# Hybrid SSD / MLA / PEER block on one core: one gate multiplication per build step, and a later decode of the gathered token block

## The chip, the cores and the metric

The kernel runs on one core of a Trainium2 chip. The engines of the core are named as the profile names them: PE (TensorE, the matrix engine; PEld is its weight load), DVE (VectorE), ACT (ScalarE), POOL (GpSimd) and SP (SyncE, which here only issues DMAs). Each engine works through its own queue of instructions in order; they wait for each other through semaphores. The metric is the time of one execution on the device in microseconds, as the median of several runs.

## The reference

The model is one decoder layer for 512 tokens of width 1024: a layer norm, a mixer (16 state-space heads and 8 latent-attention heads, one input and one output projection), a second layer norm, and then the expert mixer that the change is about, followed by a third layer norm. The expert mixer, for a block of 128 tokens:

```python
q = (xb @ w_query).reshape(T, PEER_HEADS, 2, PEER_HALF_DIM)
s = jnp.einsum('thkd,hknd->thkn', q, sub_keys)
sv, si = lax.top_k(s, K)                              # K = 16 of 128, per head and half
cand_s = (sv[:, :, 0, :, None] + sv[:, :, 1, None, :]).reshape(T, PEER_HEADS, K * K)
cand_i = (si[:, :, 0, :, None] * PEER_N_KEYS + si[:, :, 1, None, :]).reshape(T, PEER_HEADS, K * K)
top_s, top_pos = lax.top_k(cand_s, K)
expert_idx = jnp.take_along_axis(cand_i, top_pos, axis=-1)
gate = jax.nn.softmax(top_s, axis=-1)
act = jax.nn.gelu(jnp.einsum('td,thkd->thk', xb, u_table[expert_idx]), approximate=False)
return jnp.einsum('thk,thkd->td', gate * act, v_table[expert_idx])
```

Each token so picks 8 x 16 = 128 of 16384 experts; expert number = 128 i + j, where i and j are the two sub-key numbers.

## The kernel before

The tokens are four blocks of 128. For blocks 0 to 2 the kernel does not gather expert rows: it multiplies all 16384 rows of both tables densely. For block 3 it gathers the picked rows from memory. The expert mixer runs in these stages.

1. **Queries and top-16** (`w_query_fm`, `sub_scores`, `stage1`, `top16`). DVE finds the 16 best sub-keys and then the 16 best candidates of every head; the results for all four blocks lie in `TS4` (scores), `PO4` (positions among the candidates) and `TI4` (sub-key numbers).
2. **Decode** (`stage2`). From a position DVE computes the pair of ranks (a, b), looks up the sub-key numbers i and j with a comparison against the table `iaE`, a multiplication with the numbers and four halving additions (L1018 to L1026, once per block, in the order 2, 0, 1, 3), and computes the softmax gate. The result of block b is `IJG[b]`: i, j and gate.
3. **Gate build** (`build_g`, 48 steps for blocks 0 to 2, eight tokens each). The wanted thing is a matrix G[expert, token] with the gates at the picked places. For one token it is the product of a one-hot matrix of j with a one-hot matrix of i that is scaled by the gates. `g_head(b)` transposes i, j and gate on PE and writes them as fp16, the gate as a high part and a low part. `hot(n)` makes the one-hots of step n on DVE with one comparison (L1111, 2048 elements per partition), multiplies the i one-hots by the low gates into `g1` (L1115, 1024 elements) and by the high gates in place (L1116, 1024 elements). PE multiplies (L1134, L1135; 16 matmuls of 128x128 a step), ACT copies the result to `stg`, and every fourth step SP writes `stg` to the DRAM buffers `gs0` and `gsp`. The one-hots of two steps and `g1` are double-buffered, and `hot(n + 1)` is issued ahead of the matmuls of step n.
4. **u and v chunks**. Chunk c is 128 experts. A *u chunk* (`u_chunk`) is the product of 128 rows of the u table with the activations of blocks 0 to 2, in three passes of split precision (`mm3`, L72 to L74; 24 matmuls), and a gelu on ACT. A *v chunk* (`v_chunk`) multiplies by G (`v_prep`, L1325, G read back through `gt`), splits the product in a high and a low part (`v_hi`, L1338; `v_lo`, L1345), and adds its 18 matmuls (L1354 to L1358) into six accumulators that stay in PSUM. The weights of both come as 512 KB pieces through `Stream`: SP loads a piece into one of three `wir` buffers, ACT rounds it to a high part (L109), DVE subtracts to get the low part (L119, "the weight split"); there are three buffers of the low part.
5. **Gather for block 3** (`gather`). POOL gathers, for each of the 128 picks, one row of u and later one row of v per token (L1391); DVE does a dot product with each u row (L1402) and adds each v row, scaled, to `ac` (L1408). It ends with the block's layer norm.

The stages overlap by a plan that is made while the program is written out. Up to 54 u chunks (`LEAD`) may be done early, their results kept in SBUF. `drive(fill)` keeps two clocks: `tm[0]` for PE (4.07 per u chunk, 1.1 per build step) and `tm[1]` for DVE (the numbers that `stage2` and `build_g` yield, and 1.2 per weight split). It puts a u chunk in as long as PE's clock is not ahead of DVE's and fewer than 52 chunks (`LEAD - RES`) are out, and otherwise takes the next piece of the filler, `stage2` or `build_g`. Sixteen tokens of block 2 are treated like block 3 for their u side: their 16 rows of u (`urow`) are multiplied on DVE in between the build steps (`ug_dots`, L1056). Chunks that are left of the 54 come behind the build. Then the main loop issues one u chunk and one v chunk at a time while u chunks remain, then v chunks alone. In each round `pump` takes pieces of `gather` worth a given time; once rows are gathered, their number follows the work that is left, so that the rows end a fixed distance before the end.

DMAs of SP go out in the order of the program and SP waits in that order; so do the instructions of each engine.

Of the kernel before, what the change touches and what calls it, by code (L numbers as in the profile page):

```python
# [53 lines left out]
def tile_block(ctx: ExitStack, tc: tile.TileContext, I, out):  # L54
# [921 lines left out]
    def stage2():  # L976
        f4 = lambda z: z.rearrange("p b h k -> p (b h k)")
        g4 = lambda z: z.rearrange("p b h k -> p (b h) k")
        d = rt2.tile([128, NB, 8, 16], F32, name="dd")
        sm = rt2.tile([128, NB * 8], F32, name="smm")  # L980
        V.tensor_tensor(g4(d), g4(TS4), g4(TS4)[:, :, 0:1].to_broadcast([128, NB * 8, 16]), op=OP.subtract)
        sm_ = lambda n, dt=F32: rt2.tile([128, NB * 128], dt, name=n)
        p3, p2, pf, a1, af, b1 = sm_("p3", U32), sm_("p2", U32), sm_("pf"), sm_("a1"), sm_("af"), sm_("b1")
        abf = rt2.tile([128, NB, 2, 128], F16, name="abf")
        ti = rt2.tile([128, NB, 2, 8, 16, 2], F16, name="tif")
        pos = f4(PO4)
        ab = lambda e: abf[:, :, e]
        v4 = lambda z: z.rearrange("p (b k) -> p b k", b=NB)
# [3 lines left out]
        yield 1.6  # L992
# [4 lines left out]
        yield 1.7  # L997
# [5 lines left out]
        yield 2.6  # L1003
# [3 lines left out]
        for b in range(NB):  # L1007
            IJG[b] = ijp.tile([128, 3, 8, 16], F32, name="ijg", bufs=4)
            V.tensor_tensor(IJG[b][:, 2], d[:, b], sm[:, b * 8:(b + 1) * 8, None].to_broadcast([128, 8, 16]), op=OP.mult)
        yield 2.0  # L1010
        sh = [128, 16, 16, 16]
        for b in (2, 0, 1, 3):
            for c in range(2):
                A.activation(ti[:, b, :, :, :, c].rearrange("p e h a -> p h e a"),
                             TI4[:, b].rearrange("p (h e) a -> p h e a", e=2), AF.Copy)
            eq = rt2.tile([128, 16, 16, 16], F16, name="eq")
            abv = abf[:, b].rearrange("p e (h k) -> p (e h) k", k=16)
            V.tensor_tensor(eq, abv[:, :, None, :].to_broadcast(sh), iaE[:, None].to_broadcast(sh), op=OP.is_equal)  # L1018
            yield 2.3
            eqv = eq.rearrange("p g a (k c) -> p (g a) k c", c=2)  # L1020
            tv = ti[:, b].rearrange("p e h a c -> p (e h a) c")
            V.tensor_tensor(eqv, eqv, tv[:, :, None, :].to_broadcast([128, 256, 8, 2]), op=OP.mult)
            yield 2.3
            for w in (8, 4, 2):
                V.tensor_tensor(eq[:, :, :w], eq[:, :, :w], eq[:, :, w:2 * w], op=OP.add)
            V.tensor_tensor(IJG[b][:, 0:2].rearrange("p e h k -> p (e h) k"), eq[:, :, 0], eq[:, :, 1], op=OP.add)  # L1026
            yield 2.8
            if b == 2:
                ug_index(p3)
            if b == 1:  # L1030
                g_head(0)

# [33 lines left out]
    def ug_head():  # L1066
# [15 lines left out]
        A.activation(gT[:, 0, 128 - UG:], ps[:, :UG], AF.Copy, scale=GSC)  # L1082
        yield 0.1
        V.scalar_tensor_tensor(gT[:, 1, 128 - UG:], ps[:, :UG], GSC, gT[:, 0, 128 - UG:],
# [3 lines left out]
    def g_head(b):  # L1088
        ijg = IJG.pop(b)
        ps = px()  # L1090
        for e in range(3):
            T.transpose(ps[:, e * 128:(e + 1) * 128], ijg[:, e].rearrange("p h k -> p (h k)"), ident)
        ijT = ijp.tile([128, 16, 2, 8], F16, name="ijT", bufs=2)
        gT = ijp.tile([128, 2, 128], F16, name="gT", bufs=2)
        A.activation(ijT.rearrange("p n e t -> p e n t"),
                     ps[:, 0:256].rearrange("p (e n t) -> p e n t", e=2, t=8), AF.Copy)
        A.activation(gT[:, 0], ps[:, 256:384], AF.Copy, scale=GSC)
        V.scalar_tensor_tensor(gT[:, 1], ps[:, 256:384], GSC, gT[:, 0], op0=OP.mult, op1=OP.subtract)
        GT[b] = ijT, gT

    def build_g():
        bc = [128, 4, 128, 2]

        def hot(n):
            ijT, gT = GT[n // 16]
            t0 = n % 16 * 8
            col = lambda z: z[:, t0:t0 + 8].rearrange("p (q c) -> p q c", c=2)[:, :, None, :].to_broadcast(bc)
            ij = gb.tile([128, 2, 4, 128, 2], F16, name="ij", bufs=2)
            g1 = gb.tile(bc, F16, name="g1", bufs=2)
            b2 = [128, 8, 128, 2]  # L1110
            V.tensor_tensor(ij.rearrange("p e q i c -> p (e q) i c"), iotaE[:, None].to_broadcast(b2),  # L1111
                            ijT[:, n % 16].rearrange("p e (q c) -> p (e q) c", c=2)[:, :, None, :].to_broadcast(b2),
                            op=OP.is_equal)
            oi, oj = ij[:, 0], ij[:, 1]
            V.tensor_tensor(g1, oi, col(gT[:, 1]), op=OP.mult)  # L1115
            V.tensor_tensor(oi, oi, col(gT[:, 0]), op=OP.mult)  # L1116
            return oj, oi, g1
# [5 lines left out]
        for n in range(48):  # L1123
# [25 lines left out]
            yield 2.55 if n < 47 else 0.1  # L1149
# [70 lines left out]
    iaE = ijp.tile([128, 16, 16], F16, name="iaE")  # L1220
    nc.sync.dma_start(iotaE.rearrange("p a b -> p (a b)"), I["ch"][:, 0:256])
    nc.sync.dma_start(iaE.rearrange("p a b -> p (a b)"), I["ch"][:, 256:512])
# [60 lines left out]
    rt2 = pool("rt2")  # L1283
    lo_on[0] = V
# [85 lines left out]
    def gather():  # L1370
        ijg = IJG.pop(3)
# [5 lines left out]
        close(ijp)  # L1377
# [56 lines left out]
    while vc <= LASTC:  # L1434
# [11 lines left out]
        if GS[0] < 0:  # L1446
            more = pump(fill, 1.7 * w)
# [153 lines left out]
```

## Time and profile before

| | |
|---|---|
| median of 3 runs | 1629.04 us (1628.13 to 1629.44) |
| profiled execution, its own time | 1628.98 us |
| its span, first to last instruction | 1627.1 us |
| PE busy | 1584.2 us (97%) |
| PE weight load busy | 1395.5 us (86%) |
| DVE busy | 1363.0 us (84%) |
| ACT busy | 704.9 us (43%) |
| POOL busy | 465.7 us (29%) |
| moved by DMA | 394.82 MB, mean 243 GB/s |

In the rows of the profile, `L1111` is line 1111 of the kernel before, then come engine, operation, and output<-inputs by the names of the tiles (shortened, and without buffer numbers: `ij` is the one-hot tile, `g` the tile `g1`, `wih` and `wil` the high and low parts of the weights, `va` the accumulators). A row of the timeline begins with the start and the duration in us; in square brackets stands how long the engine had been idle and what ended the wait. The decode lies at 549 to 600 us of the profiled execution, the build at 600 to 785, the first v chunk at 799, the gathered rows from 818 to 1550.

### The profile page before, as it was taken

The page shows a single profiled execution, that of the slowest core. Times are in us where ns is not written, and L with a number is a line of the kernel's source. Part 1 is how long each engine was busy: PE and PEld are TensorE (multiplying, and loading weights), DVE is VectorE, ACT ScalarE, POOL GpSimd, SP SyncE. Part 2 cuts the span into 40 slices and gives each one's busy share as a digit, 9 for nine tenths or more (in the row PEclk, how much of TensorE's full clock was granted, in tenths as well). Part 3 has the DMA queues.
Part 4 walks back from the last instruction along what each step waited for, and adds up shares of the span by engine and source line. Part 5 has one row for each costly group of instructions (what it writes and reads, how often), then busy time and mean ns, then how long its engine had stood idle before and what let it go on. Part 6 is the DMA issues. An engine that isn't in the chain of part 4 may idle for free.

```text
span 1627.1 us, 23774 instructions
## 1 busy us (share of the span) xinstructions
PE 1584.2 (97%) x8640; PEld 1395.5 (86%) x8640; DVE 1363.0 (84%) x2597; ACT 704.9 (43%) x1225; POOL 465.7 (29%) x340
## 2 busy tenths in 40 slices
PE   7999999999999999999899999999999999999997
PEld 5777878888888999998899999999999999888886
DVE  8978677747799999999588888788888888998977
ACT  5575467641433545555433333343333333333341
POOL 0000010000143213200145555555454454533300
PEclk9999999999999999999999999999999999999999
DMA  6242122364432458766799999999999999999972
GB/s 245 91 157 91 46 77 58 113 234 142 135 92 87 121 183 294 286 236 245 253 366 350 348 322 347 341 345 335 336 353 340 340 331 351 359 340 337 332 231 116
DMA packets 151245, 394.82 MB, mean 243 GB/s; under 512 B 12665, under 2 KB 64713, under 8 KB 149337
## 3 DMA queue, kind: packets, MB, share of 16 engines
q1 hardware_dynamic: 107400, 237.76, 42.9%
q0 software_dynamic: 43584, 155.29, 26.3%
q8 instruction: 67, 1.10, 0.3%
q14 instruction: 50, 0.40, 0.1%
q10 hardware_dynamic: 144, 0.26, 0.0%
HBM read 359.66 MB, written 31.51 MB: 240 GB/s over the span
## 4 chain that ended last, share of the span: by engine, by line
PE 71%; DVE 21%; ACT 3%; DMA 2%; issue 2%; SPq 0%; DVEq 0%; ACTq 0%
PE va L1354 10%; PE va L1358 10%; PE va L1355 10%; PE pu L72 7%; PE pu L74 7%; PE pu L73 7%; DVE wil L119 3%; PE pa L72 3%; PE pa L74 3%; PE pa L73 3%; DVE ij L1111 2%; DVE g L1115 1%; DVE t L955 1%; PE pw L73 1%; PE pw L74 1%
## 5 line engine op out<-in xcount | busy, mean ns | idle before, releaser
L109 ACT ACTIVATE wih<-wir 128x1024 fp32r<-128x1024 f32 (+2 forms) x269 | 277.9, 1034 | 256.7 <-DMA wir<-v 95.1
L119 DVE TENSOR_TENSOR wil<-wir,wih 128x1024 fp32r<-128x1024 f32 (+1 forms) x254 | 302.1, 1190 | 103.5 <-ACT wih L109 48.7
L74 PE MATMUL pu<-XTH,wil 128*128 128x368 f32 x1008 | 331.7, 329 | 0.7 <-DVE wil L119 0.7
L72 PE MATMUL pu<-XTH,wih 128*128 128x368 f32 x904 | 298.9, 331 | 0.0
L73 PE MATMUL pu<-XTL,wih 128*128 128x368 f32 x904 | 296.8, 328 | 0.0
L1355 PE MATMUL va<-wil,Ph 128*128 128x512 f32 x726 | 283.4, 390 | 0.0
L1391 POOL DMA_INDIRECT row<-u,ix x128 | 185.9, 1452 | 232.3 <-DVE row L1402 138.6
L1391 POOL DMA_INDIRECT row<-v,ix x128 | 181.3, 1416 | 197.3 <-DVE ac L1408 169.1
L74 PEld LDWEIGHTS pu<-XTH,wil 128*128 128x128 f32 x1008 | 189.1, 188 | 1.3 <-DVE wil L119 1.3
L72 PEld LDWEIGHTS pu<-XTH,wih 128*128 128x128 f32 x904 | 169.6, 188 | 2.9
L73 PEld LDWEIGHTS pu<-XTL,wih 128*128 128x128 f32 x904 | 169.5, 187 | 2.9
L1354 PE MATMUL va<-wih,Ph 128*128 128x512 f32 x432 | 168.5, 390 | 0.0
L1408 DVE SCALAR_TENSOR_TENSOR ac<-row,hd,ac 128x1024 f32<-128x1024 f32 x128 | 164.0, 1281 | 3.0 <-DMA row<-v,ix 0.8
L1207 ACT ACTIVATE act<-pu 128x368 f32<-128x368 f32 x126 | 60.0, 476 | 231.2 <-PE pu L74 231.1
L1355 PEld LDWEIGHTS va<-wil,Ph 128*128 128x128 f32 x726 | 136.8, 188 | 26.1
L1402 DVE SCALAR_TENSOR_TENSOR row<-row,x 128x1024 f32<-128x1024 f32 x128 | 150.3, 1220 | 1.6 <-DMA row<-u,ix 1.5
L109 ACT ACTIVATE wihx<-wir 128x1024 fp32r<-128x1024 f32 x67 | 71.1, 1061 | 155.4 <-DMA wir<-v 121.9
L1358 PE MATMUL va<-wih,Pl 128*128 128x512 f32 x432 | 133.3, 390 | 0.0
L119 DVE TENSOR_TENSOR wil<-wir,wihx 128x1024 fp32r<-128x1024 f32 x62 | 75.8, 1223 | 52.2 <-issue 49.6
L1354 PE MATMUL va<-wihx,Ph 128*128 128x512 f32 x294 | 115.6, 393 | 1.9 <-ACT Ph L1338 1.9
L1358 PEld LDWEIGHTS va<-wih,Pl 128*128 128x128 f32 x432 | 81.1, 188 | 17.3
L1354 PEld LDWEIGHTS va<-wih,Ph 128*128 128x128 f32 x432 | 81.1, 188 | 15.7
(459 smaller groups left out, 3074.6 us busy)
## 6 DMA issues: line engine op xcount, KB each, us to landing
wir<-ut SPq DMA_DIRECT2D x128, 512.0 KB, 5.5
wir<-v SPq DMA_DIRECT2D x128, 512.0 KB, 6.6
gsp<-stg SPq DMA_DIRECT2D x12, 1920.0 KB, 7.1
gt<-gsp SPq DMA_DIRECT2D x30, 768.0 KB, 10.2
wir<-wo SPq DMA_DIRECT2D x26, 512.0 KB, 3.6
wir<-wf SPq DMA_DIRECT2D x18, 512.0 KB, 3.3
wir<-wqr SPq DMA_DIRECT2D x16, 512.0 KB, 3.6
de<-acd POOLq DMA_DIRECT2D x8, 512.0 KB, 5.3
```

The source lines that it names most:

```text
L72: T.matmul(ps, lh, rh, start=start, stop=False)
L73: T.matmul(ps, lh, rl, start=False, stop=False)
L74: T.matmul(ps, ll, rh, start=False, stop=stop)
L109: A.activation(h, r, AF.Copy)
L119: self.lo(n).tensor_tensor(l, r, h, op=OP.subtract)
L1207: A.activation(ACT[c][:, :NU], ps, AF.Gelu)
L1354: T.matmul(va[b][e], Ph[:, bs], h[:, cs], start=c == 0, stop=False)
L1355: T.matmul(va[b][e], Ph[:, bs], l[:, cs], start=False, stop=False)
L1358: T.matmul(va[b][e], Pl[:, bs], h[:, cs], start=False, stop=c == 127)
L1391: G.indirect_dma_start(out=R[s], out_offset=None, in_=I["u"] if s < 128 else I["v"], in_offset=bass.IndirectOffsetOnAxis(ap=ix[:, s % 128: ...
L1402: V.scalar_tensor_tensor(r, r, 1.0, x3, op0=OP.mult, op1=OP.mult, accum_out=hd[:, s:s + 1])
L1408: V.scalar_tensor_tensor(ac, r, hd[:, s - 128:s - 127], ac, op0=OP.mult, op1=OP.add)
```

## The change

The build step keeps its comparison, but makes one multiplication: the i one-hots (read twice) times the high and the low gates, 2048 elements into a new double-buffered tile `g`. The gate tile `gT` is laid out so that high and low gates of a step lie side by side. The one-hots of all steps share three slots: the middle one holds i, the outer two hold j in turn; so `ijT` is stored in the order i, j for even steps and j, i for odd ones, for which `g_head` makes four transposes in place of three and two copies in place of one. The planned cost of a step falls from 2.55 to 2.42.

The body of `stage2` becomes `decode`, which runs once for blocks 2, 0, 1 ahead of the build, with smaller planned costs, and once for block 3 at the start of `gather` (`late3`), in a pool of its own. For this, three DMAs at the start of `stage2` write block 3's scores, positions and numbers to DRAM, and `late3` issues four DMAs that read them and the table `iaE` back. `iaE` is loaded first behind the top-16 stage, not ahead of it. Until rows are gathered, `pump` may take pieces worth 2.1 per chunk in place of 1.7.

```diff
+    t3d = [dram.tile([128, n, 16], dt, name=nm) for n, dt, nm in ((8, F32, "ts3"), (8, U32, "po3"), (16, U32, "ti3"))]
+
+    def decode(p, TS, PO, TI, ia, blocks, nb):
...
-        for b in (2, 0, 1, 3):
+        for b in ((2, 0, 1) if nb > 1 else (0,)):
             for c in range(2):
-                A.activation(ti[:, b, :, :, :, c].rearrange("p e h a -> p h e a"),
-                             TI4[:, b].rearrange("p (h e) a -> p h e a", e=2), AF.Copy)
+                A.activation(ti[:, :, :, :, c].rearrange("p e h a -> p h e a"),
+                             TI[:, b].rearrange("p (h e) a -> p h e a", e=2), AF.Copy)
...
+    def stage2():
+        for dst, t in zip(t3d, (TS4, PO4, TI4)):
+            nc.sync.dma_start(dst, t[:, 3])
+        yield from decode(rt2, TS4[:, :3], PO4[:, :3], TI4[:, :3], iaE, (0, 1, 2), 3)
+
+    late = []
+
+    def late3():
+        lt = pool("lt", side="right")
+        t = [lt.tile([128, 1, n, 16], dt, name=nm) for n, dt, nm in ((8, F32, "ts"), (8, U32, "po"), (16, U32, "ti"))]
+        ia = lt.tile([128, 16, 16], F16, name="iaE")
+        nc.sync.dma_start(ia.rearrange("p a b -> p (a b)"), I["ch"][:, 256:512])
+        for z, src in zip(t, t3d):
+            nc.sync.dma_start(z[:, 0], src)
+        yield 3.4
+        yield from decode(lt, *t, ia, (3,), 1)
+        late.append(lt)
...
     def g_head(b):
         ijg = IJG.pop(b)
         ps = px()
-        for e in range(3):
-            T.transpose(ps[:, e * 128:(e + 1) * 128], ijg[:, e].rearrange("p h k -> p (h k)"), ident)
-        ijT = ijp.tile([128, 16, 2, 8], F16, name="ijT", bufs=2)
-        gT = ijp.tile([128, 2, 128], F16, name="gT", bufs=2)
+        for x, e in enumerate((0, 1, 0, 2)):
+            T.transpose(ps[:, x * 128:(x + 1) * 128], ijg[:, e].rearrange("p h k -> p (h k)"), ident)
+        ijT = ijp.tile([128, 8, 2, 2, 8], F16, name="ijT", bufs=2)
+        gT = ijp.tile([128, 16, 2, 8], F16, name="gT", bufs=2)
...
     def build_g():
-        bc = [128, 4, 128, 2]
+        jij = gb.tile([128, 3, 4, 128, 2], F16, name="ij")
 
         def hot(n):
             ijT, gT = GT[n // 16]
-            t0 = n % 16 * 8
-            col = lambda z: z[:, t0:t0 + 8].rearrange("p (q c) -> p q c", c=2)[:, :, None, :].to_broadcast(bc)
-            ij = gb.tile([128, 2, 4, 128, 2], F16, name="ij", bufs=2)
-            g1 = gb.tile(bc, F16, name="g1", bufs=2)
+            r = n % 2
+            col = ijT[:, n % 16 // 2, r].rearrange("p e (q c) -> p (e q) c", c=2)
             b2 = [128, 8, 128, 2]
-            V.tensor_tensor(ij.rearrange("p e q i c -> p (e q) i c"), iotaE[:, None].to_broadcast(b2),
-                            ijT[:, n % 16].rearrange("p e (q c) -> p (e q) c", c=2)[:, :, None, :].to_broadcast(b2),
-                            op=OP.is_equal)
-            oi, oj = ij[:, 0], ij[:, 1]
-            V.tensor_tensor(g1, oi, col(gT[:, 1]), op=OP.mult)
-            V.tensor_tensor(oi, oi, col(gT[:, 0]), op=OP.mult)
-            return oj, oi, g1
+            V.tensor_tensor(jij[:, 1 - r:3 - r].rearrange("p e q i c -> p (e q) i c"), iotaE[:, None].to_broadcast(b2),
+                            col[:, :, None, :].to_broadcast(b2), op=OP.is_equal)
+            g = gb.tile([128, 2, 4, 128, 2], F16, name="g", bufs=2)
+            b4 = [128, 2, 4, 128, 2]
+            gv = gT[:, n % 16].rearrange("p e (q c) -> p e q c", c=2)
+            V.tensor_tensor(g, jij[:, 1][:, None].to_broadcast(b4), gv[:, :, :, None, :].to_broadcast(b4), op=OP.mult)
+            return jij[:, 2 - 2 * r], g[:, 0], g[:, 1]
...
-            yield 2.55 if n < 47 else 0.1
+            yield 2.42 if n < 47 else 0.1
...
     def gather():
+        yield from late3()
         ijg = IJG.pop(3)
...
-        close(ijp)
+        close(*late, ijp)
...
         if GS[0] < 0:
-            more = pump(fill, 1.7 * w)
+            more = pump(fill, 2.1 * w)
```

More of the change, by code (lines that the diff above doesn't have):

```diff
@@ L991, in stage2 @@
         V.tensor_copy(pf, pos)
-        yield 1.6
+        yield 1.2 if nb > 1 else 0.6
         V.tensor_scalar(a1, p3, -1.0, 0.0, op0=OP.add, op1=OP.max)
@@ L996, in stage2 @@
         V.tensor_scalar(b1, af, 4.0, 24.0, op0=OP.mult, op1=OP.add)
-        yield 1.7
+        yield 1.3 if nb > 1 else 0.7
         V.tensor_copy(ab(0), v4(af))
@@ L1002, in stage2 @@
         V.tensor_tensor(ab(1), v4(pf), v4(b1), op=OP.add)
-        yield 2.6
+        yield 2.0 if nb > 1 else 1.0
         A.activation(f4(d), f4(d), AF.Exp)
@@ L1025, in stage2 @@
                 V.tensor_tensor(eq[:, :, :w], eq[:, :, :w], eq[:, :, w:2 * w], op=OP.add)
-            V.tensor_tensor(IJG[b][:, 0:2].rearrange("p e h k -> p (e h) k"), eq[:, :, 0], eq[:, :, 1], op=OP.add)
+            V.tensor_tensor(IJG[blocks[b]][:, 0:2].rearrange("p e h k -> p (e h) k"), eq[:, :, 0], eq[:, :, 1], op=OP.add)
             yield 2.8
-            if b == 2:
+            if nb > 1 and b == 2:
                 ug_index(p3)
-            if b == 1:
+            if nb > 1 and b == 1:
                 g_head(0)
+    def stage2():
[13 more added lines that the diff above has]
+        late.append(lt)
     GT, UR = {}, {}
@@ L1081, in ug_head @@
         gT = GT[2][1]
[L1082 removed]
+        gv = ps[:, :UG].rearrange("p (n t) -> p n t", t=8)
+        A.activation(gT[:, 16 - UG // 8:, 0], gv, AF.Copy, scale=GSC)
         yield 0.1
[L1084 removed]
+        V.scalar_tensor_tensor(gT[:, 16 - UG // 8:, 1], gv, GSC, gT[:, 16 - UG // 8:, 0],
                                op0=OP.mult, op1=OP.subtract)
@@ new lines, in g_head @@
+        ijT = ijp.tile([128, 8, 2, 2, 8], F16, name="ijT", bufs=2)
+        gT = ijp.tile([128, 16, 2, 8], F16, name="gT", bufs=2)
+        gv = ps[:, 384:512].rearrange("p (n t) -> p n t", t=8)
+        for r in range(2):
+            src = bass.AP(tensor=ps.tensor, offset=ps.offset + r * 136, ap=[ps.ap[0], [128, 2], [16, 8], [1, 8]])
+            A.activation(ijT[:, :, r].rearrange("p n e t -> p e n t"), src, AF.Copy)
+        A.activation(gT[:, :, 0], gv, AF.Copy, scale=GSC)
+        V.scalar_tensor_tensor(gT[:, :, 1], gv, GSC, gT[:, :, 0], op0=OP.mult, op1=OP.subtract)
@@ L1283, in tile_block @@
     rt2 = pool("rt2")
+    iaE = rt2.tile([128, 16, 16], F16, name="iaE")
+    nc.sync.dma_start(iaE.rearrange("p a b -> p (a b)"), I["ch"][:, 256:512])
     lo_on[0] = V
```

39 lines of the change are left out of this document (17 added, 22 removed).

## The prediction

> **What bounds the kernel now.** First the page: the span, and the second line of the chain that ended last.
>
> ```profile
> span 1627.1 us, 23774 instructions
> ...
> PE va L1354 10%; PE va L1358 10%; PE va L1355 10%; PE pu L72 7%; PE pu L74 7%; PE pu L73 7%; DVE wil L119 3%; PE pa L72 3%; PE pa L74 3%; PE pa L73 3%; DVE ij L1111 2%; DVE g L1115 1%; DVE t L955 1%; PE pw L73 1%; PE pw L74 1%
> ```
>
> TensorE (PE) carries the chain; VectorE (DVE) enters it through the one-hots of the gate build (L1111, L1115). The profiled execution took 1628.98 us against a median of 1629.04, so the sum below, made on this trace, needs no correction. Second, the busy time by stage (columns: stretch in us, its length, busy of PE, PE weight load, DVE, ACT, POOL, granted clock, DMA share, GB/s).
>
> ```profile
> 600.00:690.00 90.00, 88.94 (x723) 86.16 (x722) 88.71 (x110) 48.04 (x93) 22.53 (x14) 1.00 0.76 276
> 690.00:724.00 34.00, 31.96 (x307) 30.25 (x305) 32.40 (x38) 19.97 (x41) 0.53 (x1) 1.00 0.72 256
> 724.00:787.00 63.00, 57.03 (x523) 54.22 (x521) 58.30 (x72) 35.37 (x69) 0.48 (x1) 1.00 0.63 223
> 787.00:818.00 31.00, 29.07 (x151) 26.72 (x149) 13.43 (x19) 10.94 (x20) 6.12 (x5) 0.94 0.88 301
> 818.00:1170.00 352.00, 352.00 (x1823) 320.13 (x1822) 289.96 (x428) 131.72 (x217) 183.96 (x126) 1.00 0.96 344
> 1170.00:1550.00 380.00, 380.00 (x1853) 333.26 (x1852) 333.36 (x358) 141.18 (x217) 178.24 (x128) 1.00 0.97 341
> ```
>
> The first three rows are the build: DVE is over 90% busy, PE stands idle 1.1, 2.0 and 6.0 us. From 818 to 1550 PE has no gap, so PE work there is the floor and DVE, at 82 and 88%, has room. What an edit of the build can gain is therefore PE's idle time before 805 and nothing else. Third, what PE waited for from 600 to 806 (total us, times, longest).
>
> ```profile
> PE pw L1134 <- DVE ij L1116: 7.7, 8, 1.5
> PE va L1354 <- ACT Ph L1338: 1.9, 1, 1.9
> PE pw L1134 <- ACT stg L1137: 1.4, 6, 0.2
> ```
>
> So 7.7 + 1.4 = 9.1 us in the build and 1.9 behind it: 11.0 us. Fourth, PE's instructions around one such wait, and at the start of the V stage; then two stretches there.
>
> ```profile
> 691.66 0.23 PE L1134 MATMUL pw<-ij 128*128 128x128 f16 x1 [1.14 <-DVE ij L1116]
> ...
> 692.56 0.41 PE L72 MATMUL pu<-XTH,wih 128*128 128x368 f32 x1
> 692.81 0.33 PE L73 MATMUL pu<-XTL,wih 128*128 128x368 f32 x1
> ...
> 696.65 0.23 PE L1134 MATMUL pw<-ij 128*128 128x128 f16 x1
> ```
>
> ```profile
> 796.91 0.33 PE L74 MATMUL pu<-XTH,wil 128*128 128x368 f32 x1
> 799.17 0.74 PE L1354 MATMUL va<-wihx,Ph 128*128 128x512 f32 x1 [1.93 <-ACT Ph L1338]
> ...
> 803.61 0.39 PE L1354 MATMUL va<-wihx,Ph 128*128 128x512 f32 x1
> 803.84 0.39 PE L1355 MATMUL va<-wil,Ph 128*128 128x512 f32 x1
> ...
> 804.97 0.33 PE L72 MATMUL pu<-XTH,wih 128*128 128x368 f32 x1
> ```
>
> ```profile
> 785.00:799.10 14.10, 12.24 (x75) 11.93 (x72) 1.94 (x3) 4.39 (x9) 0.00 (x0) 1.00 0.93 289
> ```
>
> ```profile
> 799.10:805.00 5.90, 5.83 (x19) 4.69 (x20) 4.98 (x9) 3.43 (x7) 0.00 (x0) 0.71 0.54 181
> ```
>
> A build step costs PE 692.56 − 691.66 = 0.90, a u chunk 696.65 − 692.56 = 4.09. The first v chunk waits 1.9 us and then runs at a granted clock of 0.71: it takes 804.97 − 799.17 = 5.8 us, where 18 matmuls 0.23 apart make 4.1. The gap thus costs 1.9 + 1.7 = 3.6 us. It is the gate's way through DRAM: only three u chunks cover it, because the planner had issued 52 of its 54 early chunks before the last four build steps, which therefore stand bare.
>
> **The change, part by part.** How many chunks and splits stand where is read from the two built programs' order. (a) One multiplication. DVE starts around the first step, the last step's last instruction, and what DVE itself waited for:
>
> ```profile
> 600.81 1.22 DVE L1111 TENSOR_TENSOR ij<-iotaE,ijT 128x2048 f16<-128x2048 f16 x1
> 602.07 0.69 DVE L1115 TENSOR_TENSOR g<-ij,gT 128x1024 f16<-128x1024 f16 x1
> ...
> 603.40 1.22 DVE L119 TENSOR_TENSOR wil<-wir,wih 128x1024 fp32r<-128x1024 f32 x1
> 604.54 1.21 DVE L119 TENSOR_TENSOR wil<-wir,wihx 128x1024 fp32r<-128x1024 f32 x1
> ...
> 783.33 0.69 DVE L1116 TENSOR_TENSOR ij<-ij,gT 128x1024 f16<-128x1024 f16 x1
> ```
>
> ```profile
> DVE ij L1111 <- PE pw L1135: 1.3, 1, 1.3
> DVE gT L1098 <- ACT gT L1097: 1.0, 1, 1.0
> ```
>
> Start to start, a step is 1.26 + 1.33 = 2.59. The new product has 2048 fp16 elements with L1111's broadcast pattern, so I give it L1111's 1.22, which lets an independent successor start after 1.14, as 603.40 to 604.54 shows. The step becomes 1.26 + 1.14 = 2.40: 0.19 x 48 = 9.1 us. Against this, twelve comparisons directly follow the product that reads their shared slot, and must now wait for its end: 0.1 x 12 = 1.2. Net 7.9 us of DVE. Bounds: zero, if the merged product costs the old pair's 1.33, and 9.1. I take 7.9; element count, type and pattern are a row's own.
>
> [...]
>
> (b) Decoding of block 3 leaves the stage ahead of the build.
>
> ```profile
> 548.70 0.68 DVE L981 TENSOR_TENSOR dd<-ts 128x512 f32<-128x512 f32 x1
> ...
> 559.07 1.22 DVE L119 TENSOR_TENSOR wil<-wir,wihx 128x1024 fp32r<-128x1024 f32 x1
> ```
>
> ```profile
> L1025 DVE TENSOR_TENSOR eq<-eq 128x2048 f16<-128x2048 f16 (+2 forms) x12 | 9.3, 778 | 0.3
> L1022 DVE TENSOR_TENSOR eq<-eq,tif 128x4096 f16<-128x4096 f16 x4 | 9.1, 2282 | 0.0
> L1018 DVE TENSOR_TENSOR eq<-abf,iaE 128x4096 f16<-128x4096 f16 x4 | 9.1, 2282 | 0.0
> ...
> L1026 DVE TENSOR_TENSOR ijg<-eq 128x256 f32<-128x256 f16 x4 | 1.7, 424 | 0.1
> ```
>
> One block's look-up is (9.3 + 9.1 + 9.1 + 1.7) / 4 = 7.3 us. The common front is 559.07 − 548.70 = 10.4 less two weight splits of 1.14, 8.1; three quarters of its width saves at most 2.0, I take 1.6 as the instruction count stays. DVE: −8.9.
>
> (c) What DVE's shorter run does to the order. The planner now issues 48 u chunks before the last step, so 45 weight splits ahead of it become 40: −5 x 1.14 = −5.7. DVE's last step ended at 783.33 + 0.69 = 784.0. After: 784.0 − 7.9 − 8.9 − 5.7 = 761.5, or 759.2 if its 2.3 us of waits go too. PE's last step then ends at 760.1 to 762.4. PE's own work for that point: the last step ended near 785.0; less 9.1 waits and 4 x 4.09 = 16.4 it is 759.5, plus 0.3 at most for three added 128x128 transposes. Both engines come out together, so some waits remain where two steps stand without a chunk; I take 762.0 (2.2 us of waits left). Bounds: 759.8 with none; 766 with 6 us, two thirds of the 9.1.
>
> (d) Then seven u chunks (six kept back, one of the main loop) cover the gate's way through DRAM: 7 x 4.0 = 28.1 us, where before 785.0 to 799.17 was 14.2. The first v chunk starts at 790.1 without wait, at full clock, and ends at 794.2, before at 804.97. Gain 10.8 us.
>
> [...]
>
> (e) The moved decode and its transfers.
>
> ```profile
> wir<-v SPq DMA_DIRECT2D x5, 512.0 KB, 6.7
> ...
> gt<-gs SPq DMA_DIRECT2D x2, 768.0 KB, 11.0
> ...
> gs<-stg SPq DMA_DIRECT2D x1, 128.0 KB, 1.7
> ```
>
> ```profile
> 551.55 0.33 SPq L91 DMA_DIRECT2D wir<-ut  x1
> ```
>
> SP gets three spill DMAs that wait for the last top-16 (548.7) and at some 0.4 us each are issued before its next weight load at 551.55: nothing. The reload of the one-hot table issues earlier, behind no wait: nothing. Late, four small loads stand on SP behind a weight load, and DVE's first decode instruction waits for them with the next weight split queued behind it. That split must land before PE is through three chunks (about 12.2 us) after the buffer's release. Ahead of it lie the split before (1.1), issue (1.0), the landing, eight narrow instructions (about 2.3) and its own 1.1: 5.5 plus the landing, so up to 6.7 is covered. The landing is between 1.7 (128 KB) and 11.0 (the pair of gate loads); nearest is the load it queues behind, 6.7. I take 0.3 us; at 11.0 PE would stall 4.3 and perhaps pay another 1.7 of clock, 6. The Exp adds two ACT table loads in a stage where ACT is 37% busy: hidden. The look-up and its front, at most 7.3 + 8.1 = 15.4 us of DVE, lie in iterations that carry no gathered rows yet; without that cover they would cost PE that much at worst.
>
> (f) The gather's first row now follows three chunk pairs later, 24 us of PE; its pace is set from the work left, so it packs 3.0 instead of 2.9 rows per pair (by the built program's order) and ends at the same place. DVE has 18% to spare: nothing.
>
> Sum: 1628.98 − 10.8 + 0.3 = **1618.5 us**.
>
> **Rivals.** *The decode's loads stall the V stage*: 11.0 us to land, price 6, time 1624.5. For it: DMA is 88% busy there. Against: the late loads are small and no gather runs yet.
>
> *The gain is given back to the DMA engines.* They are 96 to 97% busy from 818 on. If 344 GB/s were their limit, three pairs without gather (9 rows of 512 KB, 4.7 MB) would lose 13.7 us, more than the gain: 1632. It decides only if the limit is reached. Against it stands
>
> ```profile
> 809.00:818.00 9.00, 9.00 (x48) 8.10 (x46) 4.06 (x5) 3.84 (x7) 2.81 (x3) 1.00 0.96 374
> ```
>
> 374 GB/s at the same share.
>
> [...]
>
> *It doesn't do what it says*: a product at the old pair's 1.33. DVE ends at 784.0 − 8.9 − 5.7 = 769.4, or 767.1 without its waits; PE's last step at about 769, the first v chunk at 801.2: gain 3.8, 1625.5.
>
> **How the numbers follow.** Forecast (1614.5 to 1621.5) 0.60; more waits left in the build, up to the 766 above (1621.5 to 1624), 0.12; loads stall (1624.5) 0.08; old price (1625.5) 0.05; gain given back (to 1633) 0.06; slow product 0.04; a gain beyond the sum, below 1614.5, 0.03; what I don't foresee, 0.02. The range 1614.5 to 1626 holds the first four, 0.85. A measurement here tells about 0.2%, 3.3 us, from no change. Faster than 1625.7: the first three, the gain beyond and half of the old price, 0.85; within: the rest of the old price and most of the given-back, 0.07; slower: the remainder of it, the slow product and the unforeseen, 0.08.
>
> **What would show it.** Right: the product at 1.22; DVE's wait-caused PE idle in the build at 2 to 3 us instead of 9.1; no gap and a clock of 1.00 at the first v chunk, which starts near 790; no PE gap from there to 1540. Wrong: a product above 1.4, a PE gap within 30 us behind the first v chunk, or DVE waiting for gathered rows for more than a few us.

## The result and the profile after

The changed kernel takes **1623.84 us** in the median (1623.04 to 1625.19 over eight runs), beside it the kernel before took 1628.78 us. The ratio is 0.9973, with a 95% interval of 0.9964 to 0.9983: the change makes the kernel faster by 4.9 us in the medians, where 10.5 were forecast. The sign was right and the time lies in the range; the gain is a little under half of the forecast (0.47). The profiled execution took 1623.08 us with a span of 1621.3 us, 5.8 us less than before.

First, what TensorE (PE) waited for from 584 to 830 us in the profile of the changed kernel: total us, times, longest. The product is L1139 now, the matmuls of a step L1156 and L1157, the copy to `stg` L1160.

```profile
PE pw L1157 <- DVE g L1139: 4.1, 4, 1.5
PE pw L1157 <- ACT stg L1160: 1.4, 2, 0.7
PE pu L72 <- ACT act L1230: 1.3, 2, 1.1
```

The build still waits 5.5 us, against 9.1 before. The wait of the first v chunk for `Ph` is gone; in its place a u chunk waits 1.1 us. Second, the busy time by stage, with the columns of the table in the prediction: build, kept-back u chunks, first v chunk, V stage with gathered rows.

```profile
584.00:690.00 106.00, 103.97 (x866) 100.30 (x865) 103.53 (x108) 60.19 (x119) 22.99 (x15) 1.00 0.76 271
690.00:766.60 76.60, 72.69 (x676) 69.19 (x675) 71.75 (x68) 44.13 (x89) 0.48 (x1) 1.00 0.70 248
766.60:795.00 28.40, 27.31 (x164) 27.01 (x163) 8.82 (x10) 11.02 (x22) 0.00 (x0) 1.00 0.76 241
795.00:799.20 4.20, 4.20 (x21) 3.48 (x20) 2.11 (x3) 1.84 (x3) 0.00 (x0) 1.00 0.54 161
818.00:1170.00 352.00, 352.00 (x1825) 320.25 (x1824) 291.42 (x431) 132.78 (x218) 191.81 (x129) 1.00 0.96 346
1170.00:1550.00 380.00, 380.00 (x1846) 332.61 (x1845) 335.93 (x365) 140.45 (x214) 194.05 (x129) 1.00 0.96 346
```

TensorE stands idle 2.0 and 3.9 us in the build, 1.1 us among the kept-back chunks and nowhere behind them. The first v chunk has a granted clock of 1.00 (before: 0.71). Third, the places on PE's timeline on which the comparison with the forecast rests: the longest wait of the build, the first kept-back u chunk (the end of the last step), the wait of the fifth, and the start and the end of the first v chunk.

```profile
753.60 0.23 PE L1157 MATMUL pw<-g,ij 128*128 128x128 f16 x1 [1.50 <-DVE g L1139]
...
765.61 0.41 PE L72 MATMUL pu<-XTH,wih 128*128 128x368 f32 x1
...
782.94 0.44 PE L72 MATMUL pu<-XTH,wih 128*128 128x368 f32 x1 [1.09 <-ACT act L1230]
...
795.07 0.39 PE L1377 MATMUL va<-wihx,Ph 128*128 128x512 f32 x1
...
799.16 0.33 PE L72 MATMUL pu<-XTH,wih 128*128 128x368 f32 x1
```

The first v chunk runs from 795.07 to 799.16 and ended at 804.97 before: 5.8 us, the whole difference of the spans. From its end to the last instruction it is 1621.3 − 799.16 = 822.1 us in the changed kernel and 1627.1 − 804.97 = 822.1 before. What the change gained in sum lies ahead of that point.

One part of it is chance. At 263 us TensorE waits some 1.8 us in both kernels; in the next 4 us the kernel before had a granted clock of 0.65, the changed one 1.00, in the profiled executions (the row of before, then that of after):

```profile
264.00:268.00 4.00, 3.88 (x13) 3.06 (x13) 2.09 (x6) 3.21 (x8) 0.00 (x0) 0.65 0.02 4
```

```profile
264.00:268.00 4.00, 3.55 (x21) 3.03 (x21) 2.17 (x7) 3.87 (x10) 0.00 (x0) 1.00 0.01 4
```

Of the ten profiled executions of the changed kernel and of its variants below, whose programs are the same up to there, six had the fall (a granted clock of 0.94 from 260 to 290 us) and four had not (1.00), so it comes and goes with the same instructions. The kernel before and its two variants below had it in all three of their profiled executions (0.94); so few can't tell whether they have it more often. VectorE's last candidate sum (L971), ahead of the stages that were changed, began at 456.65 instead of 457.55 (first before, then after):

```profile
457.55 0.65 DVE L971 TENSOR_TENSOR cand<-tv 128x64 f32<-128x64 f32 x3
```

```profile
456.65 0.64 DVE L971 TENSOR_TENSOR cand<-tv 128x64 f32<-128x64 f32 x3
```

That is 0.9 of the 5.8 us. What is left, 4.9, is as much as the medians give.

### The profile page after: what moved, and what is told of

Read it like the earlier page. It is cut to its first block, busy times and chain, and to the rows that moved or that the text cites. A ratio compares the mean times of both kernels' runs of the same rounds, so it can differ in the third digit from the quotient of the medians.

```text
span 1621.3 us, 23808 instructions
## 1 busy us (share of the span) xinstructions
PE 1581.0 (98%) x8643; PEld 1393.0 (86%) x8643; DVE 1357.4 (84%) x2564; ACT 708.1 (44%) x1231; POOL 481.4 (30%) x340
## 4 chain that ended last, share of the span: by engine, by line
PE 74%; DVE 18%; ACT 3%; issue 3%; DMA 2%; SPq 0%; DVEq 0%; ACTq 0%
PE va L1377 10%; PE va L1381 10%; PE va L1378 10%; PE pu L72 9%; PE pu L74 8%; PE pu L73 8%; PE pa L74 3%; PE pa L73 3%; PE pa L72 3%; DVE ij L1134 2%; DVE wil L119 2%; DVE t L955 1%; DMA wir<-ut 1%; DVE ti L959 1%; DVE ti L952 1%
## 5 line engine op out<-in xcount | busy, mean ns | idle before, releaser
L1415 POOL DMA_INDIRECT row<-u,ix x128 | 190.9, 1491 | 256.7 <-DVE row L1426 126.1
L1415 POOL DMA_INDIRECT row<-v,ix x128 | 193.8, 1514 | 168.5 <-DVE ac L1432 142.9
```

The source lines that it names most:

```text
L1415: G.indirect_dma_start(out=R[s], out_offset=None, in_=I["u"] if s < 128 else I["v"], in_offset=bass.IndirectOffsetOnAxis(ap=ix[:, s % 128: ...
```

## The experiments

**What was asked.** Why did the build keep 5.5 us of waits, and why did seven u chunks take 29.46 us (765.61 to 795.07) instead of 28.1? Theory A for the first: the order, not VectorE's speed. The planner books 1.1 us for a step on TensorE, which takes 0.90, so its clock for TensorE runs ahead and too few u chunks come between the steps. Steps then stand in pairs and triples and wait for VectorE. Behind the sixteen steps that carry rows of u, the booked costs balance at one u chunk per (4.07 − 1.2) / (2.42 − 1.1) = 2.17 steps. For that VectorE needs 2.17 x 2.40, 0.19 more for each of the 1.17 steps that directly follow another, and 1.14 for a weight split, in all 6.57 us, for what TensorE does in 4.09 + 2.17 x 0.90 = 6.05. At 0.9 a step it would be one chunk per 2.87 / 1.52 = 1.89 steps, 5.85 against 5.79. (The built program has fewer steps per chunk, since the plan books further VectorE work there: its last 31 steps stand in 16 groups, 1.94 each.) Theory L for the second: the weights of the kept-back chunks are queued, on SP and on the DMA engines, behind the last gate writes and both read-backs.

**The moved decode alone.** The changed kernel with the two multiplications and the planned step of before.

```diff
...
-            V.tensor_tensor(g, jij[:, 1][:, None].to_broadcast(b4), gv[:, :, :, None, :].to_broadcast(b4), op=OP.mult)
...
+            V.tensor_tensor(g1, oi, col(gT[:, 1]), op=OP.mult)
+            V.tensor_tensor(oi, oi, col(gT[:, 0]), op=OP.mult)
...
-            yield 2.42 if n < 47 else 0.1
+            yield 2.55 if n < 47 else 0.1
```

> The changed kernel with the two old multiplications and the old planned step of 2.55: only the decode of block 3 is moved. Theory A (what is left to gain or lose is PE's wait at steps that stand without a u chunk between them, and how many do is set by the plan's two clocks): the plan now holds 2.55 against a real 2.59, nearly as many bare steps, 50 u chunks ahead of the last step; 1623 to 1626 us, so the merged multiplication is worth 0 to 2 us. Rival B (VectorE's work sets the end of the build): the 7 us of VectorE that the merged multiplication saves come back in full, 1630 to 1631 us.

Measured: 1626.29 us, ratio 0.9990 (0.9981 to 0.9999), 0.3 us above theory A's range and far from rival B's. By the middle values some 0.1% is the moved decode's, and the merged product brings the rest, 0.9990 − 0.9973 = 0.17%, 2.8 us; the intervals are about as wide as the smaller part. The profiles split the gain the other way. Both executions were spared the fall at 264 us (granted clock 1.00), and the first v chunk ends at 800.74 here and at 799.16 in the changed kernel: 1.6 us for the product, and 804.97 − 0.9 − 800.74 = 3.3 for the decode. So both parts pay, but how they share the gain is not shown. The merged product without the moved decode was not run.

**Keeping more chunks back, without the change.** The kernel before with six chunks kept back for the end instead of two.

```diff
-RES = 2
+RES = 6
```

> The kernel before with six u chunks kept back behind the build instead of two. Theory A: eleven steps then stand bare at VectorE's 2.59 us each; the last step ends about 4.6 us earlier, but four more chunks (16.3 us) follow it, and the first v chunk ends about 7.6 us later; 1636 to 1637 us. Rival E (the gain of the change is only that more kept-back chunks cover the gates' way through DRAM, 3.6 us): 1625 to 1626 us.

Measured: 1637.66 us, ratio 1.0055 (1.0041 to 1.0068), 0.7 us above theory A's range and 12 above rival E's. Cover behind the last step is worth nothing if the build has no u chunks left for it: eleven steps stand bare, that is with no u chunk between them, at VectorE's 2.59 us each, and the clock falls as well.

```profile
762.00:800.00 38.00, 33.11 (x226) 31.26 (x225) 22.25 (x26) 16.03 (x29) 0.00 (x0) 0.71 0.68 240
```

**The planned step.** The changed kernel with a step booked as TensorE takes it.

```diff
-            tm[0] += 1.1
+            tm[0] += 0.9
```

> The changed kernel with one number of the plan altered: a build step is booked at 0.9 us on PE (measured 0.90) in place of 1.1. The order then has 51 u chunks ahead of the last step in place of 48 and no three steps in a row. Theory A: PE's waits at build steps fall from 5.5 us to about 2, PE's last step moves with the three chunks, and the first v chunk starts about 3.5 us earlier than in the changed kernel; 1619.5 to 1621 us. Rival B (VectorE's work sets the end of the build): the waits stay near 5.5 us wherever the chunks stand, 1623 to 1625 us.

Measured: 1622.29 us, ratio 0.9959 (0.9945 to 0.9973), between the two ranges; by the time alone neither theory is told from the other, nor this kernel clearly from the changed one. The profile decides. PE's waits from 584 to 830 us:

```profile
PE va L1377 <- ACT Ph L1361: 2.1, 1, 2.1
PE pw L1157 <- DVE g L1139: 0.9, 1, 0.9
PE pw L1157 <- ACT stg L1160: 0.4, 2, 0.2
```

The build's waits fell from 5.5 to 1.3 us, as theory A has it (about 2); rival B falls. But three more u chunks now stand in the build, only four behind it, and the first v chunk waits again, 2.1 us. It then also runs slowly: 792.61 to 798.43 is 5.8 us instead of 4.1. What it waits for is not the gate. VectorE had the gate product early, and ScalarE (ACT) could not convert it, since in its queue the split of the next u chunk's weights came first. The rows of VectorE, then of ScalarE:

```profile
785.91 0.56 DVE L1348 TENSOR_TENSOR P<-act,gt 128x384 f32<-128x384 f32 x1 [2.05 <-DMA gt<-gs]
```

```profile
790.62 1.06 ACT L109 ACTIVATE wih<-wir 128x1024 fp32r<-128x1024 f32 x1 [7.57 <-DMA wir<-ut]
791.59 0.20 ACT L1229 ACTIVATE act<-one 128x16 f32<-128x16 f32 x1
791.69 0.46 ACT L1230 ACTIVATE act<-pu 128x368 f32<-128x368 f32 x1
792.05 0.51 ACT L1361 ACTIVATE Ph<-P 128x384 fp32r<-128x384 f32 x1
```

**The read-backs later.** In the changed kernel SP issues behind the last step:

```profile
766.49 0.33 SPq L1164 DMA_DIRECT2D gs<-stg  x1
766.87 0.63 SPq L1165 DMA_DIRECT2D gsp<-stg  x1
768.39 3.44 SPq L1325 DMA_DIRECT2D gt<-gs  x2
771.89 4.78 SPq L91 DMA_DIRECT2D wir<-ut  x2
```

That is 2 MB of gate writes and two read-backs of 768 KB ahead of the weights of the fifth chunk, whose split on ScalarE began at 781.36 after a wait of 6.99 us. The issuing alone takes SP 3.44 and 4.78 us here; how much of the delay is SP's and how much the DMA engines' was not separated. Two edits move the read-backs. The first issues both behind the second of the kept-back chunks:

```diff
-    for q in range(2):
-        load_g(q)
     uc = un[0]
     while uc < LEAD:
         u_chunk(uc)
         uc += 1
+        if uc == un[0] + 2:
+            for q in range(2):
+                load_g(q)
+    for q in range(2):
+        load_g(q)
```

> The changed kernel with the two gate read-backs issued behind the weight loads of two of the six kept-back u chunks, not ahead of all of them. Theory C (the 1.1 us wait of PE among the kept-back chunks is for weights that queue on SP and on the DMA engines behind the last gate writes and the two read-backs): the wait goes, the first v chunk starts 28.1 us after the last step instead of 29.5, 1622.4 to 1623 us. Rival D (the DMA engines are the limit there, whatever the order): the wait moves to the first v chunk, which then waits for its gates; 1623.5 to 1626 us.

Measured: 1623.45 us, ratio 0.9971 (0.9960 to 0.9982), between the two ranges. In the profile the wait is gone: the last step ended at 767.27, the first v chunk began at 795.35, 28.1 us, 1.4 less than in the changed kernel. Its last step ended 1.7 us later than there, since this execution had the fall of the clock at 264 us (0.57) that the changed kernel's was spared; the spans, 1621.6 and 1621.3, so hide the gain. (The last two lines of the edit do nothing here: `load_g` passes over a block that it has loaded.) The second edit asks for only one block there; `v_prep` asks for the other with the first gate product:

```diff
-    for q in range(2):
-        load_g(q)
+    load_g(0)
```

> The changed kernel as it is (steps booked at 1.1) with one read-back behind the last step instead of two; the second is asked for where the V stage first needs it. Theory L: the wait of 1.09 us ahead of the fifth of the seven kept-back u chunks and the pauses beside it go, the seven take 28.1 us instead of 29.46; 1.1 to 1.4 us less than the changed kernel's 1623.8: 1622.4 to 1622.8 us. Rival: the weights are late for another cause (the gate writes of the last step, 1.9 MB): the wait stays, 1623.5 to 1624.2 us.

Measured: 1622.69 us, ratio 0.9970 (0.9961 to 0.9980), within theory L's range; in the profile the seven chunks take 28.1 us (765.34 to 793.43) and none of them waits. Against the ratio of the changed kernel, 0.9973, neither gain can be told from none; what is shown is the wait that is gone.

**Both edits together.** One read-back and the step at 0.9:

> The changed kernel with a step booked at 0.9 us in TensorE's planned time (as in the run with the planned step alone, 1622.3 us) and only the first gate block read back right behind the last step; the second block is asked for where the V stage first needs it. In the run with 0.9 alone the first gate product on VectorE began at 785.91 and ScalarE could convert it only at 792.05, because it stood for 7.57 us behind the weights of the next u chunk, which had been queued behind both read-backs (768 KB each). Theory L (weights queued behind the read-backs hold ScalarE, and with it the first v chunk): 768 KB less ahead of those weights is about 2.2 us at 350 GB/s, so the first v chunk starts about 16.5 us behind the last step instead of 18.3, with no wait long enough for the clock to drop (1.7 us more): 3.5 us less, 1618.8 us (1618 to 1619.6). Rival R (the gate's way itself, write, read-back and product, sets the start): the same as with 0.9 alone, 1622 to 1622.6 us.

Measured: **1618.46 us**, ratio 0.9943 (0.9929 to 0.9957), within theory L's range and 9.1 us under the kernel before in the same series (1627.52). It has the lowest median of all. PE's waits of 584 to 830 us, and ScalarE at the start of the V stage:

```profile
PE pw L1157 <- DVE g L1139: 1.1, 1, 1.1
PE pw L1157 <- ACT stg L1160: 0.4, 2, 0.2
```

```profile
787.75 1.06 ACT L109 ACTIVATE wih<-wir 128x1024 fp32r<-128x1024 f32 x1 [4.86 <-DMA wir<-ut]
788.71 0.20 ACT L1229 ACTIVATE act<-one 128x16 f32<-128x16 f32 x1
788.81 0.46 ACT L1230 ACTIVATE act<-pu 128x368 f32<-128x368 f32 x1
789.17 0.51 ACT L1360 ACTIVATE Ph<-P 128x384 fp32r<-128x384 f32 x1
```

With 768 KB less ahead of them the split of the weights begins 2.7 us sooner (13.6 us behind the last step instead of 16.4), the conversion follows at 789.17, and the first v chunk starts at 790.21 without a wait. By the middle values the 9.1 us are more than the sum of the parts (0.14% and 0.03% of the time for each edit alone, together 2.8 us, beside the change's 4.4 by its ratio), but the intervals are too wide to show it. What the profiles show is how the edits fit together: the plan moves chunks into the build, and the single read-back makes the four that are left enough.

Two neighbours, each with one chunk more kept back (RES = 4), with one read-back and with two:

> As the kernel with planned steps of 0.9 us and one read-back, but with one more u chunk kept back behind the last step (five instead of four, RES = 4). The last steps of the build then stand with one u chunk less and wait for VectorE: its last product ends about 1 us earlier (one weight split less), the last step about 2.2 us earlier instead of 4.1. Theory L: five u chunks (20.4 us) cover everything, the first v chunk starts with no wait, and the time is 1.6 us above that of the kernel with four: 1620.4 us (1619.8 to 1621). Rival R: five chunks cover the gate's way which four did not: 1619.5 to 1620.5 us, and then clearly less than the kernel with four (1622).

> Planned steps of 0.9 us and five u chunks kept back (RES = 4), both read-backs issued right behind the last step as in the changed kernel. Theory L: the fifth kept-back chunk waits for its weights, whose split began 16.35 us behind the last step with 0.9 alone, so it starts about 18 us behind it instead of 16.2; the wait has only moved from the first v chunk to the u chunk ahead of it, and the time is that of 0.9 alone, 1622.0 us if the clock holds, up to 1623.8 if it drops. Rival R (the gate's way sets the start): the fifth chunk covers it and the time falls to 1619.5 to 1620.5 us.

Measured: 1619.92 us, ratio 0.9950 (0.9936 to 0.9963), with one, and 1622.59 us, 0.9970 (0.9958 to 0.9982), with two. The first lies in the ranges of both theories, which overlap there; that it would be clearly less than the kernel with four, rival R's second sign, did not come. The second lies in theory L's range and is the plainest test of theory L: a fifth chunk should have covered the gate's way, and it only took over the wait: it starts 18.0 us behind the last step (772.25 to 790.28), where 18 was expected, and the v chunk behind it waits for nothing.

```profile
790.28 0.43 PE L72 MATMUL pu<-XTH,wih 128*128 128x368 f32 x1 [1.77 <-ACT act L1230]
```

**Do the two edits pay by themselves?** The kernel before with both, and the moved decode with both but with two multiplications:

> The kernel before with the same two edits that took the changed kernel to 1618.5 us: steps booked at 0.9 us and one read-back behind the last step. Theory A (the two edits pay because the change has given VectorE room; before it, VectorE's own work sets the end of the build): the build ends no earlier, its waits only move to the last nine steps, which stand with no u chunk between them; the single read-back lands about 1.4 us earlier, the first v chunk's wait of 1.93 us shrinks to about 0.5 and its clock holds (1.7 us): 3.2 us less than before, 1624 to 1625.5 us where before stands at 1628. Rival: the two edits pay by themselves, whatever the change did: the 5.4 us that they were worth to the changed kernel come here too, 1622 to 1623 us.

> The moved decode with the two edits (steps at 0.9, one read-back; RES = 3, so that four u chunks stay back as there) but with the old two multiplications, 2.59 us of VectorE a step instead of 2.40. It tells what the merged product is worth when the plan leaves little else waiting. Theory A: the last 32 steps stand on VectorE at 6.12 us for a u chunk and its 1.89 steps against TensorE's 5.79, 0.3 us for each of some 17 u chunks, less the 2 us for which VectorE is ahead at the end: 3.5 to 4.5 us above the kernel with one multiplication, 1622 to 1623 us. Rival (the product's saving is hidden, only the moved decode pays): 1618.3 to 1619.5 us.

Measured: 1632.53 us, ratio 1.0024 (1.0015 to 1.0033), and 1627.06 us, ratio 0.9992 (0.9982 to 1.0001). The rivals fall: without the merged product the two edits do not pay. Theory A's forecasts fail too, since the times lie 7 and 4 us above its ranges. For the kernel before even the direction was wrong: 3.2 us less than before was forecast, and it is 4.1 more. With two multiplications, 2.59 us a step, VectorE has no room for a denser order. It falls behind, and at the end the steps come bare: nine in a row in the first kernel, five in the second. There TensorE idles and its granted clock is lower (0.79 from 760 to 800 in the first kernel). The second kernel's bare steps, and the u chunk behind them:

```profile
774.40:781.20 6.80, 5.33 (x47) 4.81 (x48) 6.17 (x7) 2.89 (x5) 0.00 (x0) 0.51 0.53 224
781.20:787.00 5.80, 5.80 (x28) 5.80 (x27) 0.00 (x0) 1.74 (x4) 0.00 (x0) 0.69 0.70 277
```

Its last step ended at 781.3, 7.1 us later than with one multiplication (774.1), and the first u chunk took 5.7 us instead of 4.1. Chance hides a part: this execution was spared the fall at 264 us (1.00 from 260 to 290), the other was not (0.94), and at the last candidate sum it was still 1.2 us ahead (456.77 against 458.01). From there to the last step it so lost 8.4 us, where the expectation counted 3.5 to 4.5 in all, for the last 32 steps alone; why the build hid so little of VectorE's longer steps was not separated. In the kernel before the last step ended at 791.1, 6.1 us later than without the two edits, with as many u chunks ahead of it; 1.2 of these lie ahead of the last candidate sum. The part of the forecast on the first v chunk came true: its wait is 0.3 us and its clock 1.00. Under this plan, then, the merged product is worth 0.9992 − 0.9943 = 0.49%, 8.0 us, where it was worth 2.8 by the ratios under the plan that came with it.

**The first wait.** In the 1618.5 us kernel the wait of 1.1 us stands at the second step, directly behind the first. This edit, with RES = 3, puts a u chunk between them:

```diff
-            yield 2.42 if n < 47 else 0.1
+            yield (2.42 if n else 4.2) if n < 47 else 0.1
```

> The 1618.5 us kernel (changed kernel, steps at 0.9, one read-back) with the first step booked at 4.2 us of VectorE instead of 2.42 and RES = 3: one u chunk comes between the first and the second step, which stood next to each other and where TensorE waited 1.1 us for the second step's product. Theory A: that wait goes, the last steps lose one u chunk and wait a little more (0 to 1 us): 1617.4 to 1618.6 us. Rival (the first wait is VectorE's start, and only moves on): no change or slower, 1618.5 to 1619.5 us.

Measured: 1619.84 us, ratio 0.9944 (0.9930 to 0.9958), beside 0.9943: no change, as the rival has it, though the time lies 0.3 us above its range. The wait went, and the last step waits 1.5 us in its place. Build and chunks are now so nearly in balance that a chunk given at one end is missing at the other.

## Why the prediction was wrong in size

- **(a) The product.** It takes 1.22 us in all of its 48 instructions, where I gave it 1.22, and a step with a weight split behind it takes 2.40. The rivals of an old price (1.33) and of a slow product (above 1.4) fall. One term was mis-sized: a comparison that directly follows the product overwrites the slot that the product reads. It starts 1.33 behind the product's start, not 1.24.

```profile
752.32 1.22 DVE L1139 TENSOR_TENSOR g<-ij,gT 128x2048 f16<-128x2048 f16 x1
753.65 1.23 DVE L1134 TENSOR_TENSOR ij<-iotaE,ijT 128x2048 f16<-128x2048 f16 x1
754.91 1.23 DVE L1139 TENSOR_TENSOR g<-ij,gT 128x2048 f16<-128x2048 f16 x1
756.05 1.22 DVE L119 TENSOR_TENSOR wil<-wir,wih 128x1024 fp32r<-128x1024 f32 x1
757.19 1.22 DVE L1134 TENSOR_TENSOR ij<-iotaE,ijT 128x2048 f16<-128x2048 f16 x1
```

  From 752.32 to 753.65 it is 1.33, from 754.91 to 756.05 it is 1.14. For two adjacent steps the merged product thus saves nothing (1.26 + 1.33 = 2.59, the old price); the trace has fourteen such places where twelve were counted, so that is 2.7 us of VectorE instead of 1.2. The split starts 1.14 behind a product of 1.22, ahead of the product's end; the comparison, which overwrites what the product reads, starts 0.11 behind that end (752.32 + 1.22 = 753.54).
- **(b), (c) VectorE's end** was nearly right: its last product ends at 761.03 + 1.22 = 762.2, where 759.2 to 761.5 was worked out. That is 0.7 us above the range, and 1.6 without the 0.9 of chance; 1.5 of it is the adjacent steps of (a).

```profile
761.03 1.22 DVE L1139 TENSOR_TENSOR g<-ij,gT 128x2048 f16<-128x2048 f16 x1
```

- **The step that failed is the last one of (c)**: "Both engines come out together, so some waits remain [...]; I take 762.0 (2.2 us of waits left)." TensorE's last step ended at 765.61. Its own work was sized well: 759.8 plus the 5.5 us of waits that are there gives 765.3 (without the 0.9 of chance the work comes out 1.2 larger). The waits were mis-sized, 5.5 for 2.2. I had reckoned with the end of VectorE alone. But TensorE won back nothing of the 5.5 us that it waited within the build, and VectorE's balance over the whole build says nothing on how many there are; that is set by which steps stand adjacent, in pairs or triples. The order of the built program held them, and I gave them a lump instead of a price for each. The run with the step booked at 0.9 shows the cause: the same steps at VectorE's same price, with the u chunks in another order among them, and three more of them, leave 1.3 us.
- **(d) The kept-back chunks** took 29.46 us instead of 28.1, since the fifth waited 1.09 us for weights that are queued behind the gate's transfers. The prediction counted what the gate waits for, and not what waits behind the gate: the weights' place in the queue. That the first v chunk would start without a wait and at full clock (1.00), worth 3.6 us, was right; with only four chunks kept back and both read-backs it waited again (the run with the step at 0.9).
- **(e)** The late loads landed within 4.3 us of their issue, inside the 6.7 that the chunks cover. VectorE waited 5.14 us for them, and TensorE did not stall. **(f)** TensorE has no gap from 818 to 1550, at 346 GB/s with a DMA share of 0.96, and what follows the first v chunk takes as long as before: the rival in which the gain is given back to the DMA engines falls.

```profile
802.25 0.29 DVE L983 TENSOR_TENSOR dd<-ts 128x128 f32<-128x128 f32 x1 [5.14 <-DMA ts<-ts]
```

In sum: 765.6 for 762.0 is 3.6 us, 29.46 for 28.1 is 1.4, and 5.0 is what lies between the forecast end of the first v chunk (794.2) and the measured one (799.16). The forecast gain of 10.5 is missed by 5.6 in the medians; beside these 5.0 that is the 0.9 us at 263 us, which the profile of before had lost and the changed one had not, less the 0.3 of (e). The case "more waits left in the build" (0.12) is what came. That the time still lies in the stated range is owed to that case being counted in, not to the sum.

## What to carry to other kernels

When a planner interleaves two engines' work, a saving on the engine that is behind becomes time only as far as the plan's costs are true for the other engine: with a step booked at 0.9 instead of 1.1 and one read-back out of the way, the merged instruction was worth 8.0 us instead of 2.8 by the ratios. Where only that saving was missing, the same edits brought nothing (0.9992 with them, 0.9990 without), and in the kernel before they cost 4 us. Price waits by the order of the instructions, pair by pair, and not by the balance of the totals, since TensorE did not get its waits back here (5.5 us of them in the changed kernel, 1.3 with the other order). And when work is put behind a wait as cover, look at what the cover itself needs: its weights stood in the queue behind the very transfer that it was to cover.

## What was not expected of the hardware

- **Whether the clock fell after a wait was partly chance.** Behind a wait of 1.73 us at 263 us the granted clock was 0.65 in the profile of before, behind one of 1.82 at the same place 1.00 in the profile after. At the first v chunk of the kernel before it was 0.71 behind a wait of 1.93 us; behind one of 2.07, in the kernel with the step at 0.9, that chunk took 5.8 us as well, where it takes 4.1 at a clock of 1.00. Behind one of 1.77, in the kernel with five chunks kept back and both read-backs, the u chunk took 4.1 us, no longer than without a wait (790.28 to 794.39). Behind a wait of 1.50 the clock was 1.00 at 753.60 in the changed kernel, but 0.51 among the bare steps of the kernel with two multiplications. So behind waits of 1.5 to 2.1 us it fell in some places and held in others; what decides between the two was not shown.
- **A slow clock cost nothing while a step waited anyway, and was paid by what came next.** At a granted clock of 0.51 a bare step of the kernel with two multiplications kept TensorE busy for 2.59 − 0.71 = 1.88 us instead of 2.59 − 1.50 = 1.09, at no loss, for VectorE needed 2.59 (the rows show two such steps begin); the u chunk behind them then took 5.7 us, at 0.69, instead of 4.1.

```profile
774.45 0.27 PE L1156 MATMUL pw<-ij 128*128 128x128 f16 x1 [1.50 <-DVE ij L1138]
...
777.04 0.29 PE L1156 MATMUL pw<-ij 128*128 128x128 f16 x1 [0.71 <-DVE ij L1138]
```

- **One read-back less may move more than its bytes.** In the 1618.5 us kernel the DMA engines moved 312 GB/s from the last step to the first v chunk (below); 768 KB at that rate are 2.5 us by estimate. ScalarE's wait for the weights fell by about as much, from 7.57 to 4.86. The first v chunk then took 4.1 us, at a clock of 1.00, where it had taken 5.8; it ends 4.1 us earlier (794.31 instead of 798.43), in two executions that both had the fall at 264 us (0.58 and 0.60). The ratios (0.9943 and 0.9959) put it at 2.6 us, with intervals that overlap.

```profile
774.10:790.20 16.10, 16.10 (x100) 16.10 (x98) 3.49 (x5) 5.92 (x12) 0.00 (x0) 1.00 0.93 312
790.20:794.30 4.10, 4.10 (x20) 3.39 (x19) 3.51 (x6) 3.30 (x6) 0.00 (x0) 1.00 0.41 74
```
